# A hybrid encoder layer on one core: side work of attention ordered behind its scores, and four edits at the stage borders

## The chip, the cores and the metric

The kernel runs on one core of one Trainium2 chip. The metric is the device time of one execution in microseconds (us). Five engines run side by side, each with its own in-order queue: TensorE (PE, with its weight loads shown as PEld), VectorE (DVE), ScalarE (ACT), GpSimd (POOL) and SyncE (SP), which issues nearly all DMAs. 0.2% of the time is about 5.7 us.

## What is computed

One encoder layer over 2048 tokens of width 1024, in float32: an adaLN-modulated layer norm, one input projection whose columns go to grouped-query attention (8 query heads, 2 key/value heads, 64 dims) and to a convolution module, an output projection, a gated residual with layer norm, and a gated MLP with a width-3 convolution, again with residual and layer norm. What matters here:

```python
u = adaln_modulate(x, shift1, scale1)
q, k, v, glu = jnp.split(u @ w_in[l], split_cols, axis=-1)
# q, k: per-head RMS norm, axial rotary positions
attn = gqa_attention(q, k, v)          # softmax over all 2048 keys
h = a * jax.nn.sigmoid(g)              # a, g = split(glu)
h = depthwise_conv(h, conv_dw_w[l], conv_dw_b[l])        # width 31
h = layer_norm(h, conv_ln_g[l], conv_ln_b[l])
h = jax.nn.silu(h) @ w_conv_pw2[l]     # then RMS norm per channel group
mixed = jnp.concatenate([attn, h], axis=-1) @ w_o[l]
x = layer_norm(ALPHA * x + gate1 * mixed, ln1_g[l], ln1_b[l])
```

## The kernel before

The order of the work is made at compile time by a list scheduler: the program is traced in Python, the traced order is the priority, and each engine is given, by the scheduler's own estimate of time, the first traced instruction that is ready. On the chip each engine then runs its list in that order and waits where a semaphore is not there yet. `tc.issue_after(ins)` adds an order edge: what the block traces on the engine of `ins` comes after `ins` in that engine's list. All PSUM tiles are one of eight banks (`bank()`).

**Input stage.** Projections with weights split in a high and a low part (three matmuls each, `mm3`). Queries go to DRAM (`q_d`), keys stay in SBUF (`K1`), the convolution's input goes to DRAM (`h_d`).

**Attention.** 16 units: for each block of 512 queries (c) four head pairs (p). `unit_main` walks over 16 key tiles. For each it traces the scores of two heads (L574 and L575, a high and a low part; the low part also carries the negative maximum in 8 extra rows), two exponentials on ACT (L576), then calls `step()`, and every third key tile `flush()` puts the value products of three key tiles (L585) on PE. The softmax denominators are summed from the exponentials on POOL (three of four key tiles) and DVE (L606).

`step()` (L792) is where the side work is traced, one piece per key tile from generators that yield between pieces: the ends of earlier units (`unit_end`: L533, L541, a transpose), the preparation of the next unit's queries (`unit_prep`), and from unit 1 on the convolution module (`conv_work`), whose last part `load_wo` loads and splits the output projection's weights. `unit_prep` takes the maximum of the scores: 32 matmuls (L177), each followed by a DVE reduction over 512 keys (L179), then one reduction over the pieces (L182), whose result goes through a transposing matmul (L184) into the 8 extra rows (L186). Its 20th resumption does L182 and L184 together. `step()` resumes it twice in every third key tile and once in the others, and `conv_work` once:

```python
        if preps:
            drain(preps[0][0], 2 if state["n"] % 3 == 0 else 1)
        if state["unit"] > 0:
            drain(conv, 1)
```

`conv_work` has four loads of `hc` from DRAM (L657), 16 groups of depthwise convolution (ACT copy L669 into `hg`, transposes, L692), four chunks of layer norm (L98, L724 on DVE), tanh and the pointwise matmuls (three split matmuls of 512 columns, four output blocks in each chunk), and 33 resumptions of `load_wo` (DMA L627, DVE L628, ACT and DVE split). The yields come to 221 for the convolution and 33 for `load_wo`; units 1 to 15 have 240 key tiles. `second_keys` (L503) copies keys for the low part: on ACT for head group 0, on POOL for group 1.

**Output projection and first norm.** `out_mm(t)` makes 48 matmuls for 128 tokens. `load_mix(t)` loads the mixed heads of tile t (`mr`, one buffer) and splits them on ACT (`mh`) and POOL (`ml`). `norm1(t)` adds the residual (L963), takes the statistics, gets the reciprocal deviation on POOL (L91) and applies gain and bias: for t < 2 with `affine` (two DVE instructions, L105 and L106), later with `affine3` (POOL L111, ACT L112, POOL L113, DVE L114). A second statistic gives `xt` (ACT L973), and `second_in(t)` transposes it (PE L131) two tiles later. `combine` (POOL) prepares the MLP's operands from t = 10 on. The MLP runs as fast matrix products with 7 products for 8 (L1077).

The SP queue at this border has, in traced order: `xt` of tile 0, `lg`, `lb`, `xt` of tiles 1 and 2, `md` twice, `dww` (L1003), `dwb` (L1004), then `load_mix(2)` and so on.

Of the kernel before, what the change touches and what calls it, by code (L numbers as in the profile page):

```python
# [12 lines left out]
AF = mybir.ActivationFunctionType  # L13
# [8 lines left out]
NT = 16  # L22
# [11 lines left out]
def layer_kernel(ctx, tc, x, cT, w_ada, b_ada, b_adaT, w_in, qg2, kg2, rope, conv_t, cmask, mmask,  # L34
# [45 lines left out]
    def bank():  # L80
        return psp.tile([P, 512], F32, name="b", bufs=8)
# [68 lines left out]
    def unit_prep(pl, p, c, res, qpl=None):  # L150
        g = p // 2
        qd = []
        for h in range(2):
            t = (qpl or pl).tile([P, 4, 2, 64], F32, name="qd", bufs=4 if qpl else 3)
            c0 = p * P + h * 64
            for i in range(2):
                SY.dma_start(t[:, :, i, :], q_d[c * 4:(c + 1) * 4, :, c0:c0 + 64].rearrange("s b d -> b s d"))
            qd.append(t)
        pl = pl or (yield)
        yield  # L160
        mm = pl.tile([P, 8, 4], F32, name="mm", bufs=2)
        mz = pl.tile([P, 72], F32, name="mz", bufs=2)
        V.memset(mz, 0.0)
        for h in range(2):
            ps = transpose4(lambda i: qd[h][:, i].rearrange("p a d -> p (a d)"))
            q1 = pl.tile([P, 512], F32R, name="q1%d" % h, bufs=2)
            q2 = pl.tile([P, 512], F32R, name="q2%d" % h, bufs=2)
            A.activation(q1, ps, AF.Copy)
            V.tensor_tensor(q2[0:64], ps[0:64], q1[0:64].bitcast(F32), op=ALU.subtract)
            res.append((q1, q2))  # L170
            yield
        for h in range(2):
            q1 = res[h][0]
            for i in range(4):
                for kc in range(4):
                    px = bank()
                    T.matmul(px, lhsT=q1[:, i * P:(i + 1) * P], rhs=K1[:, g, kc * 512:(kc + 1) * 512],  # L177
                             start=True, stop=True)
                    V.tensor_reduce(mm[:, h * 4 + i, kc:kc + 1], px, axis=AX, op=ALU.max)  # L179
                    if kc % 2:  # L180
                        yield
        V.tensor_reduce(mz[:, 64:72], mm, axis=AX, op=ALU.max, negate=True)  # L182
        pm = bank()
        T.matmul(pm[0:72, 0:P], lhsT=mz, rhs=ident, start=True, stop=True)  # L184
        for h in range(2):
            V.tensor_tensor(res[h][1][64:72].rearrange("p (i t) -> p i t", i=4),  # L186
                            pm[64:72, 0:P].unsqueeze(1).broadcast_to([8, 4, P]),
                            mmk[64:72, h].unsqueeze(2).broadcast_to([8, 4, P]), op=ALU.mult)
        yield
# [313 lines left out]
    def second_keys(g):  # L503
        for c in range(0, S, 512):
            k1 = K1[0:64, g, c:c + 512].bitcast(F32)
            if g == 0:
                A.activation(K2[0:64, g, c:c + 512], k1, AF.Copy)
            else:
                G.tensor_scalar(K2[0:64, g, c:c + 512], k1, 1.0, 0.0, op0=ALU.mult, op1=ALU.add)
            V.tensor_copy(K2[64:72, g, c:c + 512].rearrange("p (i t) -> p i t", t=P),  # L510
                          ones[64:72].unsqueeze(1).broadcast_to([8, 4, P]))
# [48 lines left out]
    def unit_main(p, c, q, step, pvs):  # L560
        g = p // 2
        (qa1, qa2), (qb1, qb2) = q
        po = bank()
        lp = wk.tile([P, 2, 512], F32, name="lp", bufs=1)
        ld = wk.tile([P, 2, 512], F32, name="ld", bufs=1)
        first = {}
        for kt in range(NT):
            k1 = K1[:, g, kt * P:(kt + 1) * P]
            k2 = K2[0:72, g, kt * P:(kt + 1) * P]
            pr = wk.tile([P, 2, 512], F32, name="pr", bufs=6)  # L570
            for i, (m1, m2) in enumerate(((qa1, qa2), (qb1, qb2))):
                ps = bank()
                with tc.issue_after(state["pv"]) if "pv" in state else nullcontext():
                    T.matmul(ps, lhsT=k1, rhs=m1, start=True, stop=False)  # L574
                state["s"] = T.matmul(ps, lhsT=k2, rhs=m2[0:72], start=False, stop=True).ins  # L575
                ex = A.activation(pr[:, i, :], ps, AF.Exp, scale=0.125).ins  # L576
            step()
            if len(pvs) == GROUP:
                flush()

            def pv(kt=kt, pr=pr):

                for i in range(2):
                    with tc.issue_after(state["pv"]) if "pv" in state else nullcontext():
                        state["pv"] = T.matmul(po[i * 64:(i + 1) * 64, :], lhsT=vt[:, kt, g * 64:(g + 1) * 64],  # L585
                                               rhs=pr[:, i, :], start=kt == 0, stop=kt == NT - 1).ins
                    if "gate" in state:
                        tc.add_manual_dep(state["pv"], state["gate"].name, mybir.DependencyInfo(
                            mybir.DependencyClass.Sync, mybir.DependencyReason.DATA), reason="pairs")
                        tc.add_manual_dep(state["pv"], state["s"].name, mybir.DependencyInfo(  # L590
                            mybir.DependencyClass.NoSync, mybir.DependencyReason.DATA), reason="pairs")
                        del state["gate"]
                if kt == NT - 1:
                    ends.append(unit_end(p, c, po, lp, ld))

            pv.last = ex
            pvs.append(pv)
            onv = kt % 4 == 3 if (p, c) != units[-1] else kt % 4 != 1
            eng, acc, key = (V, ld, "v") if onv else (G, lp, "g")
            if key not in first:  # L600
                first[key] = pr
            elif first[key] is not None:
                eng.tensor_tensor(acc, first[key], pr, op=ALU.add)
                first[key] = None
            else:
                eng.tensor_tensor(acc, acc, pr, op=ALU.add)  # L606
# [40 lines left out]
    def conv_work():  # L647
# [14 lines left out]
        def front(g4):  # L662
            ct = c1.tile([P, 4, 48], F32, name="ct", bufs=2)
            SY.dma_start(ct, conv_t[:, g4 * 4:(g4 + 1) * 4, :])
            hT = c1.tile([P, 4, 130], F32, name="hT", bufs=2)
            G.memset(hT[:, :, 0:1], 0.0)
            G.memset(hT[:, :, 129:130], 0.0)
            hg = c1.tile([P, 4, NT, 8], F32, name="hg", bufs=2)
            A.activation(hg.rearrange("p g s c -> p s g c"),  # L669
                         hc[:, :, g4 * 32:(g4 + 1) * 32].rearrange("p s (g c) -> p s g c", c=8), AF.Copy)  # L670
            tz = c1.tile([P, 4, 48, 8], F32, name="tz", bufs=2)
            for i in range(4):
                G.tensor_tensor(tz[:, i], ct[:, i, :].unsqueeze(2).broadcast_to([P, 48, 8]),
                                cm.unsqueeze(1).broadcast_to([P, 48, 8]), op=ALU.mult)
            return hT, hg, tz
# [114 lines left out]
    pvs = []  # L790

    def step():  # L792
        for e in list(ends):
            if next(e, "end") == "end":
                ends.remove(e)
        if preps:
            drain(preps[0][0], 2 if state["n"] % 3 == 0 else 1)
        if state["unit"] > 0:
            drain(conv, 1)
        state["n"] += 1  # L800

    for i, (p, c) in enumerate(units):
# [22 lines left out]
            res.append(ps)  # L825
        return res

    pend = [out_mm(0), out_mm(1)]
    for e in ends:
        drain(e)  # L830
    ph.close()
# [127 lines left out]
    def norm1(t, pss, xt):  # L959
        z = wk.tile([P, D], F32, name="z", bufs=2)  # L960
        for n in range(2):
            sl = slice(n * 512, (n + 1) * 512)
            V.scalar_tensor_tensor(z[:, sl], xt[:, sl], ALPHA, pss[n], op0=ALU.mult, op1=ALU.add)  # L963
        mu, r = ln_stats(wk, z, "l1")
        if t < 2:
            affine(z, z, mu, r, lg, lb)
        else:
            affine3(wk, z, z, mu, r, lg, lb, "l1")
        SY.dma_start(x1_d[t], z)
        mu, r = ln_stats(wk, z, "l2")  # L970
        nm = wk.tile([P, 1], F32, name="l2_n", bufs=3)
        G.tensor_scalar(nm, mu, r, -1.0, op0=ALU.mult, op1=ALU.mult)
        A.activation(xt, z, AF.Identity, scale=r, bias=nm)  # L973
# [26 lines left out]
        xs[t] = load_xt(t)  # L1000
    for i, v in enumerate((1, 2)):
        SY.dma_start(md[:, i], mod_d[v].rearrange("(k p) -> p k", p=P))
    SY.dma_start(dww, dw_w)  # L1003
    SY.dma_start(dwb, dw_b)  # L1004
    for t in range(NT):
        if t >= 2:
            pss = out_mm(t)
        else:
            pss = pend[t]
        if t + 2 < NT:  # L1010
            mixes["load"](t + 2)
        norm1(t, pss, xs[t])
        if t >= 10:
# [400 lines left out]
```

## Time and profile before

| | us |
|---|---|
| three runs | 2859.89, 2861.63, 2862.63 (median 2861.63) |
| the profiled execution, its own time | 2857.23 |
| its span, first to last instruction | 2855.4 |
| PE busy in it | 2685.8 (94%) |
| DVE, ACT, POOL busy | 2203.7, 1314.6, 1279.3 |
| mean granted TensorE clock | 0.975 of full speed |

The profile's page gives busy times, the span in 40 slices with the granted clock, and groups of instructions by line. From the trace one asks for a table by stage (busy time of each engine in a stretch, with the mean granted clock: 1.00 is 2.4 GHz, 0.50 is 1.2 GHz), for the waits of an engine (who waited for whom, in total, how often, the longest), for groups by line in a stretch, and for the timeline of an engine. Input stage: 0 to 402 us; attention: to 1248; output projection and first norm: to about 1470; MLP: the rest.

### The profile page before, as it was taken

The numbers are of one execution on the slowest core, as the hardware profiler recorded it, in microseconds if no ns is written. First come the engines' busy times: TensorE is split into PE (matmuls) and PEld (weight loads), VectorE is DVE, ScalarE is ACT, GpSimd is POOL, SyncE is SP. The second block draws the span as 40 slices with busy tenths as digits, with TensorE's granted clock in tenths as the row PEclk, the third lists the DMA queues.
The fourth block names the chain that finished last, engine by engine and source line by source line (L and its number), as shares of the span: only waits on it lengthen the run. The fifth ranks groups of instructions, "written<-read, shape, count | busy, mean of one in ns | idle before, by whom it ended". The sixth has DMA issues, their size and how long they took to land. (4 is left out here: it accounts for less than half of the span.)

```text
span 2855.4 us, 35234 instructions
## 1 busy us (share of the span) xinstructions
PE 2685.8 (94%) x12108; PEld 2021.2 (71%) x12108; DVE 2203.7 (77%) x3174; ACT 1314.6 (46%) x2578; POOL 1279.3 (45%) x940
## 2 busy tenths in 40 slices
PE   7999989999999999989988999999999999999996
PEld 6877765665556655557766888877788887776774
DVE  7554466668677677674578999989999888989988
ACT  4333324445454544534564545455445555443542
POOL 3543437868567676624755222324322002335234
PEclk8999999999999999989999999999999999999998
DMA  8343241010011010135767433545444236545542
GB/s 271 95 138 114 79 98 23 25 30 19 23 27 30 19 26 23 56 101 173 230 194 237 139 126 122 166 125 160 148 135 141 74 108 210 155 130 152 164 139 65
DMA packets 336869, 320.59 MB, mean 112 GB/s; under 512 B 70689, under 2 KB 244129, under 8 KB 336689
## 3 DMA queue, kind: packets, MB, share of 16 engines
q1 hardware_dynamic: 336688, 318.34, 37.2%
q8 instruction: 95, 1.56, 0.2%
q14 instruction: 86, 0.70, 0.1%
HBM read 225.71 MB, written 92.55 MB: 111 GB/s over the span
## 5 line engine op out<-in xcount | busy, mean ns | idle before, releaser
L1077 PE MATMUL b<-o,wh 128*128 128x512 f32 x3696 | 1155.5, 397 | 54.6 <-ACT wh L123 20.4
L1077 PEld LDWEIGHTS b<-o,wh 128*128 128x128 f32 x3696 | 698.1, 190 | 227.3 <-ACT wh L123 28.7
L1077 PE MATMUL b<-o,wl 128*128 128x512 f32 x1848 | 717.7, 396 | 14.9 <-DVE wl L126 14.8
L179 DVE TENSOR_REDUCE mm<-b 128x1 f32<-128x512 f32 x512 | 323.8, 681 | 142.7 <-PE b L177 140.1
L1077 PEld LDWEIGHTS b<-o,wl 128*128 128x128 f32 x1848 | 350.5, 190 | 100.3 <-DVE wl L126 21.3
L606 POOL TENSOR_TENSOR lp<-lp,pr 128x1024 f32<-128x1024 f32 x152 | 378.8, 2492 | 84.9 <-ACT pr L576 77.8
L576 ACT ACTIVATE pr<-b 128x512 f32<-128x512 f32 x512 | 280.2, 598 | 295.3 <-PE b L575 290.3
L123 ACT ACTIVATE wh<-wr 128x512 fp32r<-128x512 f32 (+2 forms) x456 | 250.6, 569 | 342.9 <-PE b L1077 205.2
L126 DVE TENSOR_TENSOR wl<-wr,wh 128x512 fp32r<-128x512 f32 (+2 forms) x456 | 336.2, 748 | 16.9 <-ACT wh L123 16.7
L585 PE MATMUL b<-pr,vt 128*64 128x512 f32 x1024 | 245.6, 614 | 1.8 <-ACT pr L576 1.6
L1174 POOL TENSOR_TENSOR cb<-cb,g 128x512 f32<-128x512 f32 x44 | 89.5, 2050 | 335.0 <-DMA cb<-in_w_down_dram 326.5
L574 PE MATMUL b<-q,K 128*128 128x512 f32 x512 | 218.2, 429 | 2.6 <-DVE mm L179 2.1
L575 PE MATMUL b<-q,K 72*128 72x512 f32 x512 | 205.2, 404 | 0.0
L177 PE MATMUL b<-K,q 128*128 128x512 f32 x512 | 170.6, 419 | 15.1 <-ACT pr L576 9.2
L585 PEld LDWEIGHTS b<-pr,vt 128*64 128x64 f32 x1024 | 67.1, 139 | 131.3 <-issue 111.8
L126 POOL TENSOR_TENSOR o<-stg,o 128x512 fp32r<-128x512 f32 x53 | 86.9, 1640 | 152.0 <-ACT o L123 139.8
L177 PEld LDWEIGHTS b<-K,q 128*128 128x128 f32 x512 | 90.5, 190 | 85.7 <-issue 45.6
L123 ACT ACTIVATE o<-stg 128x512 fp32r<-128x512 f32 x177 | 106.7, 627 | 82.6 <-DMA stg<-w_d 47.1
L1054 POOL TENSOR_TENSOR wr<-wr,wr 128x384 f32<-128x384 f32 (+1 forms) x32 | 34.7, 1083 | 238.8 <-DMA wr<-g_d 165.1
L574 PEld LDWEIGHTS b<-q,K 128*128 128x128 f32 x512 | 99.0, 194 | 41.8 <-issue 15.9
L575 PEld LDWEIGHTS b<-q,K 72*128 72x128 f32 x512 | 99.5, 195 | 16.7
L126 DVE TENSOR_TENSOR o<-stg,o 128x512 fp32r<-128x512 f32 x124 | 100.8, 836 | 6.1 <-ACT o L123 6.1
(262 smaller groups left out, 4934.0 us busy)
## 6 DMA issues: line engine op xcount, KB each, us to landing
wr<-in_w_up_dram SPq DMA_DIRECT2D x88, 512.0 KB
stg<-w_d SPq DMA_DIRECT2D x133, 256.0 KB
g_d<-y SPq DMA_DIRECT2D x44, 512.0 KB
w_d<-cb SPq DMA_DIRECT2D x77, 256.0 KB
wr<-g_d SPq DMA_DIRECT2D x96, 192.0 KB
ar<-in_w_ada_dram SPq DMA_DIRECT2D x64, 256.0 KB
cb<-in_w_down_dram SPq DMA_DIRECT2D x44, 256.0 KB
x<-in_x_dram SPq DMA_DIRECT2D x32, 256.0 KB
```

The source lines that it names most:

```text
L123: A.activation(hi, src, AF.Copy)
L126: (el or V).tensor_tensor(lo, src, hi.bitcast(F32), op=ALU.subtract)
L177: T.matmul(px, lhsT=q1[:, i * P:(i + 1) * P], rhs=K1[:, g, kc * 512:(kc + 1) * 512], start=True, stop=True)
L179: V.tensor_reduce(mm[:, h * 4 + i, kc:kc + 1], px, axis=AX, op=ALU.max)
L574: T.matmul(ps, lhsT=k1, rhs=m1, start=True, stop=False)
L575: state["s"] = T.matmul(ps, lhsT=k2, rhs=m2[0:72], start=False, stop=True).ins
L576: ex = A.activation(pr[:, i, :], ps, AF.Exp, scale=0.125).ins
L585: state["pv"] = T.matmul(po[i * 64:(i + 1) * 64, :], lhsT=vt[:, kt, g * 64:(g + 1) * 64], rhs=pr[:, i, :], start=kt == 0, stop=kt == NT - ...
L606: eng.tensor_tensor(acc, acc, pr, op=ALU.add)
L1054: (V if n < NU else G).tensor_tensor(a21, a11, a21, op=ALU.subtract)
L1077: T.matmul(ps, lhsT=a[x][:, k, :], rhs=b[y][k], start=first and k == 0 and (x, y) == (0, 0), stop=k == nk - 1 and x == 1, skip_group_check ...
L1174: G.tensor_tensor(b[i, k], b[i, k], g2[:, k * 512:(k + 1) * 512], op=ALU.mult)
```

## The change

```diff
@@ unit_prep @@
         V.tensor_reduce(mz[:, 64:72], mm, axis=AX, op=ALU.max, negate=True)
+        yield
+        yield
         pm = bank()
@@ second_keys @@
-            if g == 0:
+            if g == 0 and c % 1024 == 0:
                 A.activation(K2[0:64, g, c:c + 512], k1, AF.Copy)
             else:
                 G.tensor_scalar(K2[0:64, g, c:c + 512], k1, 1.0, 0.0, op0=ALU.mult, op1=ALU.add)
@@ unit_main @@
-                ex = A.activation(pr[:, i, :], ps, AF.Exp, scale=0.125).ins
+                ex = state["exp"] = A.activation(pr[:, i, :], ps, AF.Exp, scale=0.125).ins
@@ conv_work, front @@
-            A.activation(hg.rearrange("p g s c -> p s g c"),
-                         hc[:, :, g4 * 32:(g4 + 1) * 32].rearrange("p s (g c) -> p s g c", c=8), AF.Copy)
+            with tc.issue_after(state["exp"]):
+                A.activation(hg.rearrange("p g s c -> p s g c"),
+                             hc[:, :, g4 * 32:(g4 + 1) * 32].rearrange("p s (g c) -> p s g c", c=8), AF.Copy)
@@ step @@
-        for e in list(ends):
-            if next(e, "end") == "end":
-                ends.remove(e)
-        if preps:
-            drain(preps[0][0], 2 if state["n"] % 3 == 0 else 1)
-        if state["unit"] > 0:
-            drain(conv, 1)
+        with tc.issue_after(state["s"]):
+            for e in list(ends):
+                if next(e, "end") == "end":
+                    ends.remove(e)
+            if preps:
+                drain(preps[0][0], 2 if state["n"] % 2 == 0 else 1)
+            if state["unit"] > 0:
+                drain(conv, 2 if state["n"] % 6 == 0 else 1)
@@ after attention @@
-    pend = [out_mm(0), out_mm(1)]
+    pend = []
+    for t in range(2):
+        pend.append(out_mm(t))
+        mixes["load"](t + 2)
@@ norm1 @@
-        if t < 2:
-            affine(z, z, mu, r, lg, lb)
-        else:
-            affine3(wk, z, z, mu, r, lg, lb, "l1")
+        affine(z, z, mu, r, lg, lb)
@@ loop over tiles @@
-    SY.dma_start(dww, dw_w)
-    SY.dma_start(dwb, dw_b)
     for t in range(NT):
+        if t == 5:
+            SY.dma_start(dww, dw_w)
+            SY.dma_start(dwb, dw_b)
@@
-        if t + 2 < NT:
+        if 2 <= t < NT - 2:
             mixes["load"](t + 2)
```

`state["s"]` is the last score matmul traced, `state["exp"]` the last exponential. The reduction L182 stays the 20th resumption of `unit_prep`; the transposing matmul L184 becomes the 22nd. With two resumptions in every second key tile the last L177 is traced at key tile 11 and L184 at key tile 13 of each unit. With the sixth-step extra resumption of `conv_work` units 1 to 15 have 280 resumptions for the 254 yields: the convolution ends in unit 12 and `load_wo` in unit 14.

## Rows read from the trace of the kernel before

**Rows 1.** The page: busy us (share of the span) and instructions of PE.

```profile
PE 2685.8 (94%) x12108; PEld 2021.2 (71%) x12108; DVE 2203.7 (77%) x3174; ACT 1314.6 (46%) x2578; POOL 1279.3 (45%) x940
```

**Rows 2.** Table by stage: length, busy us of each engine, granted clock, DMA.

```profile
402.50:1200.00 797.50, 760.16 (x3657) 480.52 (x3656) 562.46 (x841) 381.56 (x715) 554.32 (x318) 0.98 0.13 31
1200.00:1300.00 100.00, 85.56 (x334) 55.23 (x334) 67.04 (x81) 40.64 (x74) 31.20 (x15) 0.87 0.40 114
1300.00:1470.00 170.00, 159.28 (x734) 131.30 (x733) 92.47 (x162) 90.56 (x162) 106.12 (x95) 0.97 0.71 209
...
1600.00:2855.40 1255.40, 1191.44 (x5088) 957.67 (x5086) 1147.06 (x1557) 596.15 (x1216) 372.95 (x268) 0.98 0.45 137
```

**Rows 3.** Waits of PE from 394 to 1300: total us, times, longest.

```profile
PE b L184 <- DVE mz L182: 20.4, 10, 5.2
PE b L177 <- ACT pr L576: 9.2, 1, 9.2
PE b L131 <- ACT xt L973: 6.3, 1, 6.3
PE b L541 <- DVE osq L536: 4.1, 2, 3.5
...
PE b L533 <- DVE lp L525: 2.1, 1, 2.1
...
PE b L177 <- DVE mm L179: 1.9, 3, 1.2
```

**Rows 4.** Timeline of DVE in front of one of the longest waits.

```profile
1034.41 4.68 DVE L724 TENSOR_SCALAR hc<-hc,cl_mv,cl_r 128x512 f32<-128x512 f32 x3
```

**Rows 5.** Table of stretches right after PE resumed: busy PE, PEld, DVE, ACT, POOL, granted clock.

```profile
1040.10:1045.00 4.90, 4.88 (x17) 3.99 (x18) 3.02 (x5) 2.45 (x5) 4.40 (x3) 0.53 0.00 0
1092.80:1100.00 7.20, 7.20 (x20) 3.83 (x22) 3.76 (x5) 2.39 (x4) 3.01 (x2) 0.55 0.01 2
1217.30:1226.00 8.70, 8.68 (x25) 4.13 (x25) 8.70 (x6) 4.85 (x10) 7.53 (x3) 0.52 0.39 121
1256.30:1264.00 7.70, 7.65 (x24) 6.42 (x25) 2.69 (x4) 1.95 (x4) 2.07 (x1) 0.56 0.14 39
1295.40:1302.00 6.60, 6.60 (x23) 5.59 (x24) 3.91 (x10) 4.29 (x10) 3.87 (x5) 0.60 0.76 222
```

**Rows 6.** Timeline of ACT in unit 0.

```profile
432.13 1.15 ACT L669 ACTIVATE hg<-hc 128x512 f32<-128x512 f32 x2 [13.18 <-issue]
```

**Rows 7.** Groups by line from 1190 to 1265: busy us, mean ns, idle before.

```profile
L126 DVE TENSOR_TENSOR wol<-rw,woh 128x512 fp32r<-128x512 f32 x16 | 15.0, 954 | 0.2
L628 DVE TENSOR_TENSOR rw<-rw,row_g 128x512 f32<-128x512 f32 x16 | 12.1, 758 | 9.8 <-DMA rw<-in_w_o_dram 9.8
```

**Rows 8.** Table by stage: unit 0, which has no convolution work.

```profile
402.50:455.10 52.60, 40.20 (x168) 23.13 (x166) 33.73 (x52) 22.51 (x41) 37.50 (x27) 0.90 0.57 108
```

**Rows 9.** Timeline of all engines at the start of the first norm.

```profile
1277.63 5.16 SPq L1003 DMA_DIRECT2D dww<-in_dw_w_dram  x1
...
1290.43 2.34 POOL L126 TENSOR_TENSOR ml<-mr,mh 128x1024 fp32r<-128x1024 f32 x1 [10.40 <-ACT mh L123]
1292.73 1.06 POOL L91 TENSOR_TENSOR l_r<-l_e,mhalf 128x1 f32<-128x1 f32 x2
```

**Rows 10.** Waits of PE from 1300 to 1470.

```profile
PE b L131 <- ACT xt L973: 6.5, 3, 3.7
```

**Rows 11.** Groups by line from 1270 to 1490: the two forms of the affine step.

```profile
L113 POOL TENSOR_TENSOR z<-z,lg 128x1024 f32<-128x1024 f32 x14 | 34.2, 2444 | 23.0 <-ACT z L112 22.8
L112 ACT ACTIVATE z<-z,l_n,l_r 128x1024 f32<-128x1024 f32 x14 | 17.2, 1232 | 8.2 <-POOL l_n L111 8.2
L105 DVE SCALAR_TENSOR_TENSOR z<-z,l_mv,lg 128x1024 f32<-128x1024 f32 x2 | 2.6, 1276 | 0.0
```

**Rows 12.** Line L114: duration ns least/median/most, first and last start us.

```profile
L114 DVE TENSOR_TENSOR z<-z,lb x14: 1206/1226/2295, 1306.5 to 1482.9; 128x1024 f32<-128x1024 f32 x14
```

**Rows 13.** The page's group of the exponentials: busy us, mean ns, idle before.

```profile
L576 ACT ACTIVATE pr<-b 128x512 f32<-128x512 f32 x512 | 280.2, 598 | 295.3 <-PE b L575 290.3
```

## The prediction

> **What bounds the kernel now.** I began with the page: PE is busy for 94% of the span, no other engine for more than 77% [rows 1]. So what the change is worth is what it takes from PE's idle time and from the stretches at half clock. The table by stage says where these lie [rows 2]. Attention (402.5 to 1200) has 37 us of idle PE in 797.5; the border behind it 14.4 us in 100, at a mean granted clock of 0.87; output projection and norm 10.7 us in 170. Of the rest only the first tens of microseconds after 1470 can feel the change; the 1255 us from 1600 on, with 64 us idle, are not touched.
>
> Third, who ended PE's waits [rows 3]. The largest term is L184, the matmul that transposes the maxima, on DVE's L182: 20.4 us in 10 waits, up to 5.2. PE stands there because the last matmuls whose maxima L182 collects are the ones just before it. In front of one long wait DVE worked off three normalisations L724 in 4.68 us [rows 4], with one last L179 behind them. Then one wait of 9.2 us for the exponentials, which is not ACT being slow: in the timeline ACT stands at the first L669, the copy out of `hc`, 13.2 us until 432.13 [rows 6], with exponentials queued behind it; the `hc` DMAs had not landed.
>
> Fourth, the clock behind the waits. After five waits PE resumed at 0.52 to 0.60 granted [rows 5], 1.2 GHz for most of the stretch, 2.4 GHz later. Work lost in a stretch is (1 - clock) times its length: 2.3, 3.2, 4.2, 3.4 and 2.6 us.
>
> **The change part by part,** against the profiled execution: span 2855.4, own time 2857.2, 4.4 below the median of 2861.6.
>
> *Maxima.* The two yields put L184 two resumptions behind L182, and the last L177 (key tile 11) two key tiles ahead of L184 (key tile 13). A unit without convolution keeps PE 40.2 us for 16 key tiles [rows 8], 2.5 us each, so DVE gets at least 5 us more, about the longest wait. The 8 rows are needed only in the next unit, two key tiles on. One of the ten waits (2.1 us, before attention) I give back: there L184 moves behind a projection, right before the first scores that need it. Removed: 20.4 - 2.1 = 18.3, and 2.3 + 3.2 of half clock [rows 5]: **23.8**. Bounds 12 (DVE late by more than two key tiles) and 26.
>
> *The copy behind the exponential.* L669 now follows unit 1's first exponential, 20 us after `hc` is in. The 9.2 us go [rows 3]. The first transposes then wait for exponential and copy, two instructions of 0.6 us each [rows 6, 13]: **8**. Bounds 6 and 11.
>
> *Second keys.* Two of four copies move from ACT to POOL, which has time in unit 0 (37.5 of 52.6 us busy [rows 8]). The first exponential may come 1 us earlier and L186 1 us later: **0**, bounds -2 and +2.
>
> *`load_wo` inside attention.* Before, its DVE work, 16 x (0.76 + 0.95) = 27 us [rows 7], ran with unit 15 and the first output tile, and delayed L541, L533 and the split weights. After, it is over in unit 14. I take out L541's 4.1 and L533's 2.1 [rows 3] and the half clock behind both, 4.2 + 3.4 [rows 5]: 13.8. But the 27 us now lie in units 12 to 14, over 28 key tiles, beside the maxima. A bare unit asks 33.7 us of DVE against 40.2 of PE [rows 8]; 16/28 of 27 makes 15.7 more, 49 against 40. So DVE may be 9 us late in each of 1.75 units, 16 us. The quiet last key tiles and the banks absorb part; I take 7. Sum **6.8**, bounds -2 and +14.
>
> *Mix tiles early, `dww` late.* Issuing `dww` held SP 5.16 us, and with it the load of mix tile 3; POOL's split of that tile (2.34) then stood in front of two L91 [rows 9] that the first `xt` waits for. This chain is PE's 6.3 us [rows 3] and 2.6 of half clock [rows 5]. After, tile 3 is issued before these; the chain ends some 7 us sooner. `dww` meets nobody at t = 5, where the load is two tiles ahead. **8.9**, bounds 3 and 9.
>
> *`affine`.* Per tile DVE gets 2 x 1.28 us [rows 11] for L114's 1.23 [rows 12], 14 x 1.33 = 18.6 in all; POOL loses 2.44 and ACT 1.23. The serial chain of a tile loses some 4 us. From 1300 to 1470 DVE is busy 92 of 170 us, POOL 106 [rows 2], so I expect the three waits of 6.5 us [rows 10] to go and DVE's extra work to be covered: **6.5**. Bounds -6 (if a third of 18.6 reaches the path) and +12 (the MLP's start gains too).
>
> *Order behind the scores, denser steps.* Followed through PE's timeline, the maxima's matmuls already stand behind their scores; only some pointwise and depthwise pieces ran a key tile ahead. Where such filling is lost, PE may wait for two exponentials, 1.2 us [rows 13]; at 16 output blocks that is 19 us. I take 5, since ACT idles 290 us waiting for scores [rows 13] and the banks are mostly free. Two convolution pieces in every sixth step press DVE's norms together: 3, bounds 0 and 10. Together **-8**, bounds -29 and 0.
>
> Sum: 23.8 + 8 + 0 + 6.8 + 8.9 + 6.5 - 8 = 46.0 us. 2857.2 - 46.0 = 2811.2; at the median's level 2861.6 - 46 = **2815.6**.
>
> **The rivals.** *DVE keeps the waits.* DVE is what is late; then PE meets the same backlog one instruction later, at a bank that a reduction has not freed (L177 on L179, 1.9 us now [rows 3]). Then the maxima give 8 instead of 23.8 and `load_wo` 0 instead of 6.8: 46 - 22.6 = 23.4, 2838. For it: the 49 against 40 us above. Against it: over attention DVE has 235 idle us [rows 2].
>
> *The affine step is held by POOL.* L114 took 1.23 us in the median but up to 2.30 [rows 12]: it reads two SBUF operands while POOL works. If each of the 28 new DVE instructions is held by 1.07, that is 30 us more on top of 18.6. DVE has 78 idle us there [rows 2], so only the part near the MLP's start counts, about a third, 16: the term turns from 6.5 to -10, the sum to 29.5, 2832. The Trainium skill (SBUF — State Buffer, "two separate sides") states that a DVE instruction with two SBUF inputs and a GpSimd instruction that reads SBUF exclude each other for a whole instruction. By that rule the two new instructions are exposed as L114 was; the trace's 2.30 beside 1.23 agrees.
>
> *Scores first starves PE (slower).* Place: every key tile of units 1 to 15, 240 of them. If side work can no longer fill the time until the exponentials free a bank, PE stands. The 54 us of gains without the last term are used up at 0.23 us per key tile; at 0.3 it is 72, 18 slower: 2880. Against it: most side work is already in that order, and two exponentials are shorter than 2.5 us of PE work.
>
> **How the numbers follow.** Forecast 0.60; DVE keeps the waits 0.17; affine held 0.13; PE starved 0.10. The forecast's own range takes the terms' nearer bounds, 2795 to 2830; with the first two rivals and bad bounds of two terms together the range is **2793 to 2852**. A measurement tells 0.2%, 5.7 us, from no change. Faster: 0.60 + 0.13 + 0.12 of the first rival's 0.17 = 0.85; the other 0.05 same; slower 0.10.
>
> **What would show it.** Right: L184's waits on L182 under 4 us in total; no ACT wait at L669; no L628 after unit 14; the first L131 wait under 2 us; attention's clock near 1.00. Wrong: long waits of L177 or L574 on L179 in units 12 to 14 (first rival), DVE instructions of L105 and L106 well over 1.28 us and PE waiting on L973 (second), PE waiting on L576 in most key tiles (third). The forecast fails if the MLP's first 130 us lengthen by what the norm stage gains.

## The result, and the profile after

The changed kernel took 2837.88 us in the median of four runs (2836.24 to 2841.01), the kernel before, on the same chip, 2862.13: a ratio of 0.9923 (95% interval 0.991 to 0.9936), 24.3 us faster. The forecast was 2815.6, 46 us faster: right sign, half the size. The time lies above the forecast's own range (2795 to 2830) and inside the wide one (2793 to 2852).

The page after, its line of PE; [rows 1] has the one before:

```profile
PE 2682.2 (94%) x12108; PEld 2019.5 (71%) x12108; DVE 2229.9 (79%) x3188; ACT 1296.5 (46%) x2562; POOL 1252.0 (44%) x914
```

The table by stage (columns as in [rows 2]), cut at the events themselves: first to last score of attention, last score to last output projection, the MLP's first column block, the rest of its first half, its second half. Before:

```profile
402.48:1240.37 837.89, 796.47 (x3798) 499.35 (x3797) 595.52 (x871) 406.27 (x760) 571.00 (x324) 0.97 0.14 35
1240.37:1460.05 219.68, 202.79 (x907) 163.35 (x906) 116.53 (x196) 102.45 (x180) 118.58 (x101) 0.95 0.65 187
1460.05:1498.69 38.64, 28.22 (x111) 21.93 (x109) 34.24 (x51) 24.96 (x51) 12.32 (x11) 0.82 0.52 156
```

and after:

```profile
402.49:1240.92 838.43, 796.45 (x3800) 499.39 (x3798) 604.52 (x888) 410.73 (x768) 576.16 (x327) 0.98 0.15 36
1240.92:1445.01 204.09, 196.72 (x907) 159.83 (x906) 132.16 (x194) 79.10 (x152) 93.44 (x75) 0.98 0.66 192
1445.01:1481.68 36.67, 27.12 (x110) 21.53 (x109) 30.57 (x49) 24.28 (x50) 8.74 (x9) 0.86 0.59 179
```

Attention, where most of the 30.6 us of four terms (23.8 + 8 + 6.8 - 8) should have appeared, gained nothing: 837.9 and 838.4. The border gained 15.6 and the MLP's start 2.0. The two profiled executions differ by 16.3 in span, less than the medians' 24.3: the one after was the slowest of its four runs, the one before faster than its median. Four executions of one program spread over some 5 us here and over 13 in experiment 3, ten over 18 in experiment 9, so what follows is read from stages of a few tens of us.

Yet the waits that the change aimed at did go. Waits of PE from 394 to 1300, after ([rows 3] before):

```profile
PE b L186 <- DVE mz L182: 7.8, 5, 2.6
PE b L695 <- DVE q L169: 6.5, 1, 6.5
PE b L576 <- DVE mm L179: 5.5, 4, 2.9
PE b L177 <- DVE mm L179: 5.2, 3, 2.2
PE b L587 <- ACT pr L578: 4.9, 5, 2.5
PE b L576 <- ACT pr L578: 3.1, 1, 3.1
...
PE b L131 <- ACT xt L977: 2.6, 1, 2.6
```

L186 is L184 of before: 20.4 us in ten waits became 7.8 in five, and the wait of 9.2 us at the exponential is gone from unit 0. In their place stands one wait of 6.5 at L695 (a depthwise matmul, in unit 1), L576 and L177 (a score and a matmul of the maxima) wait 10.7 us for reductions, 6.6 of it in unit 13, and L576 and L587 (value products) wait 8.0 for exponentials, 5.5 of it in unit 14. What this costs is seen unit by unit (a unit runs from its first score to the next unit's). Before, units 1, 13, 14 and 15 (unit 0 is [rows 8]):

```profile
455.10:512.17 57.07, 57.07 (x329) 40.32 (x327) 35.98 (x63) 25.47 (x49) 41.25 (x40) 1.00 0.08 22
1100.70:1153.81 53.11, 53.11 (x250) 34.75 (x249) 29.94 (x46) 24.25 (x45) 28.94 (x12) 1.00 0.04 11
1153.81:1200.48 46.67, 45.30 (x213) 27.53 (x212) 32.84 (x48) 22.89 (x44) 31.64 (x12) 1.00 0.16 46
1200.48:1240.32 39.84, 35.76 (x139) 18.41 (x139) 32.88 (x30) 24.16 (x45) 16.67 (x6) 0.87 0.34 105
```

After, units 0, 1, 13, 14 and 15:

```profile
402.49:444.82 42.33, 38.67 (x169) 22.53 (x167) 32.08 (x54) 20.56 (x37) 29.37 (x26) 1.00 0.71 134
444.82:515.69 70.87, 62.17 (x356) 44.80 (x355) 37.36 (x68) 27.00 (x52) 53.99 (x46) 0.95 0.07 19
1099.42:1158.76 59.34, 49.89 (x185) 27.63 (x184) 56.45 (x63) 27.34 (x49) 36.30 (x15) 0.86 0.28 86
1158.76:1208.55 49.79, 44.00 (x184) 24.21 (x182) 41.23 (x55) 24.04 (x46) 27.59 (x12) 0.93 0.10 32
1208.55:1240.92 32.37, 31.41 (x140) 16.82 (x138) 15.84 (x13) 18.36 (x37) 13.03 (x6) 1.00 0.02 9
```

Unit 0 is 10.3 us shorter and unit 1 is 13.8 longer, with 27 more matmuls of the denser convolution (without these it is 8.0, experiment 5). Unit 13 has 185 matmuls where it had 250 (the convolution is over earlier) and takes 6.2 us longer; DVE is busy for 56.5 of its 59.3 us. Two theories came from this (the letters in the expectations below have the meaning that each gives them): **A**, `load_wo`'s DVE work beside the maxima costs what the thinner maxima waits and unit 15 gain, and the copy's gain in unit 0 is given back in unit 1; **B**, DVE's load as a whole keeps the waits, wherever the pieces are put.

### The profile page after: what moved, and what is told of

It is laid out like the page before. It is cut to its first block, busy times and chain, and to the rows that moved or that the text cites. A ratio compares the mean times of both kernels' runs of the same rounds, so it can differ in the third digit from the quotient of the medians.

```text
span 2839.1 us, 35217 instructions
## 1 busy us (share of the span) xinstructions
PE 2682.2 (94%) x12108; PEld 2019.5 (71%) x12108; DVE 2229.9 (79%) x3188; ACT 1296.5 (46%) x2562; POOL 1252.0 (44%) x914
## 4 chain that ended last, share of the span: by engine, by line
PE 67%; DVE 16%; issue 5%; DMA 4%; POOL 4%; ACT 2%; SPq 0%; DVEq 0%; ACTq 0%; POOLq 0%
PE b L1082 32%; PE b L587 6%; PE b L117 5%; PE b L118 5%; PE b L119 5%; PE b L177 4%; PE b L576 3%; PE b L577 3%; DVE wl L126 3%; PE b L131 2%; PE b L695 2%; POOL lp L608 1%; DVE mm L179 1%; DVE o L126 1%; DVE ac L1097 1%
## 5 line engine op out<-in xcount | busy, mean ns | idle before, releaser
L179 DVE TENSOR_REDUCE mm<-b 128x1 f32<-128x512 f32 x512 | 321.6, 682 | 113.8 <-PE b L177 112.2
L587 PE MATMUL b<-pr,vt 128*64 128x512 f32 x1024 | 244.7, 608 | 4.9 <-ACT pr L578 4.9
L576 PE MATMUL b<-q,K 128*128 128x512 f32 x512 | 218.0, 427 | 9.6 <-DVE mm L179 5.5
L177 PE MATMUL b<-K,q 128*128 128x512 f32 x512 | 165.8, 421 | 6.1 <-DVE mm L179 5.2
L587 PEld LDWEIGHTS b<-pr,vt 128*64 128x64 f32 x1024 | 66.5, 138 | 131.5 <-issue 113.4
L177 PEld LDWEIGHTS b<-K,q 128*128 128x128 f32 x512 | 92.1, 192 | 71.5 <-issue 34.1
L576 PEld LDWEIGHTS b<-q,K 128*128 128x128 f32 x512 | 99.2, 194 | 57.4 <-issue 17.8
L1097 DVE TENSOR_TENSOR ac<-b,ac 128x512 f32<-128x512 f32 x128 | 87.0, 680 | 24.0 <-PE b L1082 24.0
```

## Experiments

The kernel before took 2859.9 to 2860.2 in the three groups of runs that follow, and 2862.1 in the group of the changed kernel. A distance from the changed kernel's 2837.88 below compares medians of two groups, so some 2 us of it can be the group's.

**1. Convolution resumed once per key tile, as before; the rest of the change kept.**

```diff
-                drain(conv, 2 if state["n"] % 6 == 0 else 1)
+                drain(conv, 1)
```

> The changed kernel with one convolution piece per key tile again (no second one in every sixth). Theory A (load_wo meets the maxima on DVE in units 13 and 14 and costs some 27 us there): the idle and slow time of units 13 and 14 falls from 32 us to about 5, but load_wo runs beside unit 15 and the first output tile again and costs about 16 there; 2827 us. Theory B (the order behind the scores is what costs attention its gain, the pace moves nothing): within 4 us of the changed kernel, 2838.

Measured: 2825.12, ratio 0.988 (0.9865 to 0.9895), 12.8 us better than the change (10.5 if each is taken against the kernel before of its group): theory A. Units 13, 14 and 15:

```profile
1083.36:1138.53 55.17, 54.75 (x250) 36.12 (x249) 32.53 (x46) 23.93 (x45) 30.71 (x13) 0.97 0.04 10
1138.53:1183.60 45.07, 45.07 (x213) 27.47 (x212) 32.49 (x48) 22.95 (x44) 31.71 (x12) 1.00 0.12 33
1183.60:1224.45 40.85, 35.09 (x140) 17.38 (x138) 33.95 (x33) 25.69 (x49) 15.63 (x8) 0.92 0.41 128
```

Units 13 and 14 are again as long as before: PE is idle for 0.4 us in them, against 15.2 after the change. Unit 15 loses its 7.5 us. The three together take 141.1 us, as after the change (141.5), but with 603 matmuls for 509; the time won shows in units 1 to 12, which are rid of these 94 and take 636.5 us for 654.6. From the last score to the last output projection it takes 201.8 us, against 204.1 with `load_wo` early: the border does not need it early (in experiment 7, also without it, it took 206.9, so single executions tell no more than that).

**2. `load_wo`'s product on POOL, in the changed kernel.**

```diff
-                V.tensor_tensor(raw, raw, g1[:, sl], op=ALU.mult)
+                G.tensor_tensor(raw, raw, g1[:, sl], op=ALU.mult)
```

> The changed kernel with load_wo's 16 multiplications by the gate on POOL instead of DVE. Theory A: DVE loses 21.6 us of work in units 13 and 14, POOL has room there (36 us busy of 59, 28 of 50); most of the 27 us come back, 2818 us. Theory B: DVE is not what holds units 13 and 14; within 4 us of 2838.

Measured: 2827.77, ratio 0.99 (0.988 to 0.9919): 10 us better than the change (7.9 against the kernels before), between the two figures; its interval overlaps the change's, so it speaks against "most of the 27" and does not rule out the second figure. In the profile units 13 and 14 together are 104.8 us against 109.1. PE still waits 4.4 us at L186, and now 5.3 at L535 for DVE's L527: DVE began it at 1171.61, behind a split of 2.16 us, and took 2.28 us for it beside POOL's product, 1.23 for the same instruction in unit 13. The splits took 1558 ns in the mean, 1065 in the changed kernel. The rest of the 10 lies behind attention; why is open.

**3. `load_wo` without its work on DVE, in the changed kernel.**

```diff
-                V.tensor_tensor(raw, raw, g1[:, sl], op=ALU.mult)
...
-                split(woh[k][:, sl], wol[k][:, sl], raw)
+                A.activation(woh[k][:, sl], raw, AF.Copy)
+                A.activation(wol[k][:, sl], raw, AF.Copy)
```

> The changed kernel with load_wo's work on DVE left out: no product with the gate row, and the low part is written by ACT as a plain copy, so the output projection's weights are wrong. DVE does nothing for load_wo, the pace of all else stays. Theory: load_wo's DVE work beside the maxima is the whole of the 27 us that units 13 and 14 lost. Then their excess falls from 31.9 us to about 6, unit 13 from 59.3 to about 43, unit 14 from 49.8 to about 42, and the total from 2838 to about 2814. Rival: the loss is from the denser convolution before it (its last norms and sums fall late), and moving load_wo's work off DVE brings what moving the product alone brought, about 10: 2828.

Measured: 2813.38, ratio 0.9833 (0.9811 to 0.9854), 24.5 us better than the change (22.5 against the kernels before); this kernel leaves out the product with the gate row and the low part of the weights. Units 13 and 14 of this kernel, with all but the same matmuls as after the change:

```profile
1104.38:1148.48 44.10, 42.23 (x185) 23.83 (x184) 30.78 (x42) 37.40 (x72) 33.16 (x14) 1.00 0.47 144
1148.48:1189.16 40.68, 40.68 (x183) 23.97 (x182) 32.29 (x43) 20.46 (x40) 31.09 (x13) 1.00 0.02 7
```

59.3 + 49.8 became 44.1 + 40.7: 24.3 us, as much as the whole gain. PE is idle for 13.4 us less, and busy for 11.0 us less with the same matmuls, at a granted clock of 1.00 for 0.86 and 0.93. So `load_wo` on DVE is the cause, not the denser convolution ahead of it. How 27 us of work [rows 7] could cost as much shows in the changed kernel's groups of DVE in unit 13 (busy us, mean ns, idle before):

```profile
L179 DVE TENSOR_REDUCE mm<-b 128x1 f32<-128x512 f32 x32 | 19.9, 675 | 0.0
L630 DVE TENSOR_TENSOR rw<-rw,row_g 128x512 f32<-128x512 f32 x11 | 18.2, 1655 | 0.0
L126 DVE TENSOR_TENSOR wol<-rw,woh 128x512 fp32r<-128x512 f32 x10 | 12.9, 1292 | 0.7 <-ACT woh L123 0.7
```

The product took 758 ns in the mean before [rows 7], here 1655, the split 1292 for 954. The timeline of POOL and DVE in the same unit:

```profile
1140.22 5.13 POOL L608 TENSOR_TENSOR lp<-lp,pr 128x1024 f32<-128x1024 f32 x2 [1.84 <-ACT pr L578]
1150.57 5.13 POOL L608 TENSOR_TENSOR lp<-lp,pr 128x1024 f32<-128x1024 f32 x2 [5.22 <-ACT pr L578]
```

```profile
1143.05 2.85 DVE L630 TENSOR_TENSOR rw<-rw,row_g 128x512 f32<-128x512 f32 x1
1145.82 1.28 DVE L179 TENSOR_REDUCE mm<-b 128x1 f32<-128x512 f32 x2
...
1153.49 2.76 DVE L630 TENSOR_TENSOR rw<-rw,row_g 128x512 f32<-128x512 f32 x1
```

POOL's sums end at 1145.35 and 1155.70 (1140.22 + 5.13 and 1150.57 + 5.13); the DVE products end at 1145.90 and 1156.25, both 0.55 us later. Five of the 16 products start while one of these sums runs, and all five end so; the other eleven take 0.67 to 0.69 us, one of them beside a POOL instruction on 128x8 (1.64 us). The reductions L179, which read PSUM, take 675 ns in the mean in the same unit. So a product that meets a running POOL sum is held until the sum ends.

The holding alone does not make a unit long. In experiment 1 five of the 16 products were held too (1129 ns in the mean), in unit 15 and behind it, and unit 15 took 1.0 us more than before: it prepares no maxima, and DVE is busy for 34.0 of its 40.9 us. In unit 13 DVE has the maxima as well. No run removes the holding and leaves the work; an estimate from the rows: DVE's 30.8 us there without `load_wo` and 21 instructions at 0.68 us are 45, about the unit's 44.1, while with the held ones DVE is busy for 56.5.

In unit 14 the way to PE leads over ACT, whose `woh` needs the product and has exponentials queued behind it; ACT's timeline, then PE's:

```profile
1161.11 0.63 ACT L123 ACTIVATE woh<-rw 128x512 fp32r<-128x512 f32 x1 [3.23 <-DVE rw L630]
1163.10 0.63 ACT L123 ACTIVATE woh<-rw 128x512 fp32r<-128x512 f32 x1 [1.36 <-DVE rw L630]
1163.63 1.06 ACT L578 ACTIVATE pr<-b 128x512 f32<-128x512 f32 x2
```

```profile
1164.26 0.50 PE L576 MATMUL b<-q,K 128*128 128x512 f32 x1 [3.08 <-ACT pr L578]
```

**4. A second convolution piece in every twelfth key tile, with experiment 6's edit.**

```diff
-                drain(conv, 2 if state["n"] % 6 == 0 else 1)
+                drain(conv, 2 if state["n"] % 12 == 0 else 1)
```

> The changed kernel with the second convolution piece in every twelfth key tile instead of every sixth, and POOL's conv_t products behind the softmax sums. load_wo falls half into unit 14 and half into unit 15. If what hurts is load_wo beside the maxima, half of it costs half of the 27 us less the 7.5 that unit 15 gains: 2821.8 + 5 = 2827. Rival, that DVE has room for one piece of load_wo in unit 14 (34.8 us busy of 45.1): unit 15's gain stays, 2816.

Measured: 2824.9, ratio 0.9878 (0.9863 to 0.9893). Units 13 and 14:

```profile
1092.89:1139.61 46.72, 45.18 (x215) 27.84 (x214) 35.11 (x49) 23.60 (x44) 32.70 (x13) 1.00 0.25 68
1139.61:1199.57 59.96, 47.41 (x184) 26.41 (x182) 57.44 (x66) 29.67 (x53) 37.18 (x16) 0.90 0.23 71
```

The long unit moved with `load_wo`, from 13 to 14 (11 of the 16 products lie there). Both figures start from experiment 7's 2821.8. The time is 2 us under the first and 9 over the second, which lies outside the interval: DVE had no room for them.

**5. The order of the copy alone, on the kernel before.**

```diff
-            A.activation(hg.rearrange("p g s c -> p s g c"),
+            with tc.issue_after(state["exp"]):
+                A.activation(hg.rearrange("p g s c -> p s g c"),
```

> The kernel before with one edit, the copy into hg ordered behind the last traced exponential. Theory: unit 0 becomes some 10 us shorter (52.6 to about 43), and unit 1 gets 8 to 13 us longer, since POOL still stands at the conv_t DMA until 432 us with the softmax sums behind it, and now that wait falls into unit 1; net 2860 within 4. Rival (the forecast): the gain of 8 stays, 2852.

Measured: 2859.7, ratio 0.9998 (0.9985 to 1.001): nothing. Units 0 and 1, the latter with before's 329 matmuls:

```profile
407.35:449.64 42.29, 38.52 (x168) 22.30 (x166) 32.28 (x52) 21.60 (x39) 28.63 (x24) 1.00 0.70 134
449.64:514.68 65.04, 60.01 (x329) 42.05 (x327) 35.73 (x62) 25.68 (x50) 50.47 (x40) 0.95 0.07 19
```

10.3 us gained [rows 8], 8.0 given back at once. The changed kernel's timeline shows the way, on POOL (first the line of before), then DVE, then PE:

```profile
432.33 4.25 POOL L673 TENSOR_TENSOR tz<-ct,cm 128x384 f32<-128x384 f32 x4 [5.90 <-DMA ct<-in_conv_t_dram]
```

```profile
432.01 3.27 POOL L676 TENSOR_TENSOR tz<-ct,cm 128x384 f32<-128x384 f32 x4 [5.74 <-DMA ct<-in_conv_t_dram]
435.24 18.73 POOL L608 TENSOR_TENSOR lp<-lp,pr 128x1024 f32<-128x1024 f32 x7
```

```profile
454.00 1.23 DVE L527 TENSOR_TENSOR lp<-lp,ld 128x1024 f32<-128x1024 f32 x1 [7.11 <-POOL lp L608]
455.25 1.28 DVE L169 TENSOR_TENSOR q<-b,q 64x512 fp32r<-64x512 f32 x2
```

```profile
456.08 2.90 PE L695 MATMUL b<-tz,hT 128*128 128x128 f32 x12 [6.51 <-DVE q L169]
```

POOL stands at the DMA of the convolution's taps (`ct`) until 432.0, with seven softmax sums queued behind it. Before it stood there until 432.3, and ACT beside it at `hc` until 432.1 [rows 6]: other transfers from the same SP queue, late together. In the changed kernel POOL's last sum ends at 454.0; DVE's L527 waits 7.1 us for it, the query copies L169 behind L527 free PE's bank, and PE waits 6.5.

**6. POOL's products with the taps behind the last softmax sum traced, in the changed kernel.**

```diff
-                eng.tensor_tensor(acc, acc, pr, op=ALU.add)
+                ad = eng.tensor_tensor(acc, acc, pr, op=ALU.add)
+            if not onv and first[key] is None:
+                state["lp"] = ad.ins
...
-            for i in range(4):
+            with tc.issue_after(state["lp"]):
+                for i in range(4):
```

> The changed kernel with the POOL products of each depthwise group (tz) ordered behind the last denominator sum that POOL was given. Theory A (in unit 0 POOL stands for the conv_t DMA with the sums queued behind it, and unit 1 pays 6.5 us and half clock): unit 1's idle and slow time falls from 13 us to about 4; 2829 us. Rival (the 6.5 us come from the later hg copy itself): no change, 2838.

Measured: 2836.76, ratio 0.9921 (0.9906 to 0.9936): not to be told from the change. Unit 1 fell from 70.9 to 62.8 us, and attention from 838.4 to 830.5; in this execution the border is 2.6 us longer (206.7), and so is, by 3.6, the input stage, which the edit does not touch. The rest is inside the spread.

**7. Experiments 1 and 6 together.**

> The changed kernel with the convolution resumed once per key tile (as in the kernel before) and, in addition, POOL's conv_t products put behind the last softmax sum traced before them. Both costs of the changed kernel's attention are taken out: the crowding of units 13 and 14 (27 us of excess PE time, to about 6) and the late softmax sums in unit 1 (13 us of excess, to about 5). If the two are independent: the single edits gave about -13 (pace, 2825.1) and -1 (products, 2836.8, of which -8 inside attention was given back in unit 13); without the crowding nothing is there to take the 8 back, so 2825 - 7 = about 2818, unit 1 under 62 us. Rival, that DVE's total load and not the place of the two costs limits attention, so that any gain in unit 1 comes back later: 2825 within 3.

Measured: 2821.77, ratio 0.9865 (0.9845 to 0.9885). Units 0 and 1:

```profile
404.19:448.35 44.16, 41.14 (x170) 24.64 (x168) 32.15 (x54) 20.89 (x37) 30.54 (x21) 0.92 0.66 124
448.35:506.85 58.50, 57.71 (x329) 40.31 (x327) 34.36 (x63) 25.67 (x50) 45.19 (x43) 1.00 0.08 23
```

Unit 0 keeps 8.4 of its 10.3 us, and unit 1 is within 1.4 of before, where experiments 1 and 5, without POOL's new order, have 65.0: POOL's order was what gave the gain back. Attention is 815.3 us here and 820.9 in experiment 1; in the total that is 3.4 us, which the intervals don't separate, since the border is 5.1 longer in this execution (206.9 against 201.8). Why it differs there is open.

**8. The maxima alone, on the kernel before** (two yields, two resumptions in every second key tile).

> The kernel before with the two yields and the resumption twice in every second key tile alone. Theory A (DVE gets two key tiles and the waits are gone): 19 us less than before, 2843. Rival (DVE keeps the waits, PE meets them at the next bank): at most 8 us less, 2854 or more.

Measured: 2838.9, ratio 0.9929 (0.9914 to 0.9944), 21 us faster than before; attention 819.1. L186 waits 4.6 us in three waits.

**9. The border edits alone** (mix tiles, `dww`, `affine`), on the kernel before.

> The kernel before with the border edits alone: mix tiles issued early, dww and dwb at t = 5, affine on DVE in all tiles. No attention edit. Theory: the border edits are worth what their two terms said, 8.9 + 6.5, and do not need load_wo to be early: the stretch from the last score to the last output projection matmul shrinks from 219.6 to about 205, and the total is 2860 - 15 = 2845. Rival: the 15 us by which the changed kernel's border is shorter come from load_wo being finished in unit 14; then these edits alone give 5 or less, 2855 or more.

Measured: 2848.27, ratio 0.9956 (0.9942 to 0.9971), 11.7 us. From the last score to the last output projection 209.8 us for 219.7, the MLP's first block 34.7 for 38.6, the rest of its first half 863.3 for 866.0: 16.6 in the profiled execution, whose input stage is 4.5 us longer. So they don't need `load_wo` to be early.

**10. `affine` alone, on the kernel before.**

> The kernel before with affine on DVE in all tiles and nothing else. The forecast's term was 6.5 (bounds -6 and 12). In the changed kernel L105 took 2076 ns and L106 1514 ns in the mean against 1276 and 1286 before, 29 x 1.03 = 16 us more over 16 tiles, yet the last score to the end of the FFN's first half shrank by 16.6 in the border edits together. If the term stands: 2860 - 6.5 = 2853.5, the PE waits on xt late in the stage shorter, and the mix and dww edits are worth the other 9 to 10. Rival (the affine step is held by POOL): no gain or a loss, 2860 or more, and the whole border gain is the DMA order's.

Measured: 2852.94, ratio 0.997 (0.9959 to 0.9981), 7.2 us. The other two border edits are left with some 4.5 of the 11.7, but the two intervals (5 to 12 us here, 8 to 17 in experiment 9) overlap, so this remainder is not told from nothing, nor from the 8.9 of the forecast.

**11. The changed kernel without the order behind the scores** (`nullcontext()` in its place).

> The changed kernel without the order of the side work behind the scores; all else as changed. The forecast had 5 us of loss for this order (bounds 0 and 19). If that stands: 2833. Rival: the order decides nothing, since the matmuls concerned stand behind their scores in the list anyway: 2838 within 2. Second rival: the order is what gives the two key tiles between maxima and their use their meaning, and without it the L186 waits come back (15 us before, 8 us with the change): 2845 or more.

Measured: 2840.72, ratio 0.9932 (0.9911 to 0.9954): the change within its interval, 3 us slower by the medians and 5 against the kernels before, the wrong way for a cost. No cost of the order is seen, and it does not hold the maxima's gain.

**12. Experiment 7 with experiment 2's edit.**

> The changed kernel with the convolution resumed once per key tile, POOL's conv_t products behind the softmax sums, and load_wo's product on POOL. load_wo now lies in unit 15 and behind it, where POOL was busy for 17.6 of 40.9 us and DVE for 35.5. If DVE is what holds unit 15 (excess 11 us), the move gives some 6 us against 2821.8: 2816. Rival: POOL's products hold the DVE splits as in units 13 and 14 (L126 1558 ns against 1065), and POOL's softmax sums come late: 2822 or more.

Measured: 2818.34, ratio 0.9855 (0.9841 to 0.987). That is between the two figures, and its interval covers experiment 7's median ratio, so the two can't be told apart. Unit 15, where the gain was to come from, took 40.5 us for 40.9, and the split on DVE rose from 684 ns (experiment 1) to 1325 in the mean: there the rival was right. Both beat the kernel before, by 38 and 42 us, and the changed kernel by 16 and 19.5 (14 and 17.5 against the kernels before); experiment 3, which is faster, does less work.

## Why the prediction was half right

Beside each term what the runs gave. Experiments 5, 8, 9 and 10 are medians against the kernel before of their own group; experiments 1 and 11 against the changed kernel, in brackets through the kernels before:

| term | forecast | measured | by |
|---|---|---|---|
| maxima | 23.8 | 21 | experiment 8 |
| copy behind the exponential | 8 | 0 | experiment 5 |
| `load_wo` early, with the convolution's denser steps | 6.8 - 3 | -12.8 (-10.5) | experiment 1 |
| mix tiles, `dww`, `affine` | 8.9 + 6.5 | 11.7 | experiments 9, 10 |
| order behind the scores | -5 | 0, or 3 (5) gained | experiment 11 |

The measured column adds to 20 to 23 (22 to 27), beside 24.3. The second keys' 0 has no run of its own. The ends of the range were a judgement: the terms' bounds, added up, give 2788 to 2880.

**The step that failed** is "So DVE may be 9 us late in each of 1.75 units, 16 us. The quiet last key tiles and the banks absorb part; I take 7." Its reckoning was right in kind: DVE's need against PE's. Its price was not. It took the product and the split at 0.76 and 0.95 us, from rows of unit 15 and the border [rows 7], where POOL is busy for 16.7 of 39.8 us and one of the 16 products was held, and moved them to a unit where POOL is busy for 36.3 of 59.3. There the pair took 2.95 us. Nor were they spread over 28 key tiles: all 16 products lie between 1102.7 and 1178.1 us, 11 of them in unit 13, where 16/28 would be 9. DVE is busy for 56.5 us in unit 13 with `load_wo` and for 30.8 without (experiment 3): 25.7 more, where 15.7 were reckoned. The discount for "quiet last key tiles and the banks" was not there either: with `load_wo` unit 13 is 15.2 us longer and unit 14 9.1. Measured by experiment 3: 24.3 us for 7. On the other side of this term 13.8 were expected from unit 15 and the border; unit 15 gave 7.5 and the border nothing that shows, because without `load_wo` early it was no longer (experiment 1). The waits of L541 and L533 stood beside `load_wo`; that they came from it was only argued.

The prediction had the rule in hand and used it in the wrong place. The Trainium skill (SBUF — State Buffer, "SBUF: two separate sides") states that a DVE instruction with two SBUF inputs and a GpSimd instruction that reads SBUF exclude each other for a whole instruction. The trace agrees for the sums: none of the five products that met one ended before it, each ended 0.55 us after it; the one beside the POOL instruction on 128x8 was not held (677 ns). I weighed it for `affine` alone.

**The copy** failed at "The first transposes then wait for exponential and copy ...: 8". The wait at the exponential went as said, ACT no longer stands at the copy, and the transposes wait 0.6 us for it. What I did not follow is the other queue behind late transfers: POOL at the taps, also before. With ACT's stall gone, POOL's is what is late next: 10.3 us won in unit 0, 8.0 lost in unit 1, no change in the total (experiment 5), and with POOL's order mended as well the gain stays in attention (experiment 7).

**Right in size** were the maxima (23.8 for 21, though L186's waits did not fall under 4 us: 7.8, of which 2.6 in one wait in unit 13 behind `load_wo`) and `affine` (6.5 for 7.2). `load_wo` ended in unit 14 as reckoned. The first wait for `xt` fell from 6.3 to 2.6 us, not under 2. Attention's clock went from 0.97 to 0.98.

**The rivals.** "DVE keeps the waits" gave 2838, the measured time, but half by luck: its 8 for the maxima was wrong (21), its 0 for `load_wo` far too kind. "Affine held by POOL" was right about the instructions. Groups from 1260 to 1470, after:

```profile
L105 DVE SCALAR_TENSOR_TENSOR z<-z,l_mv,lg 128x1024 f32<-128x1024 f32 x16 | 33.2, 2076 | 0.3 <-DMA lg<-in_ln_dram 0.3
L106 DVE SCALAR_TENSOR_TENSOR z<-z,l_r,lb 128x1024 f32<-128x1024 f32 x16 | 24.2, 1514 | 19.7 <-POOL l_r L91 18.3 <-DMA lb<-in_ln_dram 1.4
```

2076 ns for 1276 [rows 11] and 1514 for 1286 (the same group before) make 16 us more over 16 tiles: 14 of the 32 took 1.9 us or more, and each of these ended 1.08 us after a POOL instruction did. The term still came out at 7.2: DVE is busy for 132 of the 204 us, and that cover held. "Scores first starves PE" found nothing (experiment 11).

**`dww` late** did not do what it says. SP's timeline after:

```profile
1264.89 0.38 SPq L637 DMA_DIRECT2D mr<-mix_d  x1
...
1274.27 5.66 SPq L1009 DMA_DIRECT2D dww<-in_dw_w_dram  x1
```

Traced at t = 5, it still stands ahead of the first `mr` of the loop, at 1281.55: it waits for nothing, and the scheduler takes the first traced instruction that is ready. What can have helped is the load at 1264.89, mix tile 3, which is now issued ahead of it; that it did is argued from the first wait for `xt`, 2.6 us for 6.3. Not tried alone: the second keys, and `dww` without the mix tiles.

## What to carry to other kernels

Price a moved instruction with rows from the place it moves to, or by what its neighbours there do to it: the same DVE product took 0.67 us alone and up to 2.87 beside POOL's sums. Spare work goes where the engine that carries it has room, so in attention the column to look at was DVE's, not PE's. When a stall on late data is removed from one queue, look for every other queue that waits for transfers issued at the same time, and put what is urgent in front of the wait there too.

## What was not expected of the hardware

How sharply the holding falls: of the 16 products of L630 in the changed kernel the shortest took 673 ns, the median 684, the longest 2866. They are either untouched or last until 0.55 us after POOL's sum ends (1.08 us for the affine instructions, on twice the columns), so their mean of 1351 is the duration of none of them, and how much a move costs depends on how often it meets a sum.
